# Third input-projection tile packed to 64 columns on two column halves, two inverses' stores moved from SyncE to GpSimd, six pieces of weight sums put into the cross-attention scores

## Chip, cores and metric

One core of a Trainium2 chip. The metric is the device time of one execution in microseconds (us): the median over runs of the whole layer, 512 tokens, model width 2048, float32 in and out.

## The reference, cut to what matters

```
h  = x
y  = rmsnorm(h) @ W_in                    # 7440 columns: GDN group and RWKV-7 group
h += concat[GDN(y_gdn), RWKV7(y_rwkv)] @ W_out
h += cross_attention(rmsnorm(h), rmsnorm(mem))   # 4 heads, 256 memory tokens
h += square(relu(rmsnorm(h) @ w_up)) @ w_down    # hidden 8192
out = rmsnorm(h)
```

Most of y's columns are queries, keys and values of the heads. A few are not: 64 + 64 + 160 low-rank columns that make RWKV's decay, its in-context rate and its output gate, and 8 + 8 columns that make GDN's decay and beta. Of the 160 gate columns 128 fill a tile; the other 32 and GDN's 16 share the next tile, 48 columns in all.

## The kernel before

Weights come in as 128-row tiles of 1024 columns (512 KB). Each is split on the chip into a high and a low float32r part (ScalarE casts the high part, VectorE subtracts), as are the activations, and a product is three fast products: high by high, high by low, low by high. The small matrices of the recurrences are multiplied in full float32, which TensorE runs as two passes and the profile lists as two records.

**Stage 1** (to 1114 us) is one program whose order is written out by a planner (`run`, with the costs of `cost` and `issue`): generators hand it instructions, and it issues the one that could start earliest by its own clocks, with ranks for ties. The engines then keep that order. `projections` makes 59 tiles of y (128 columns by 512 tokens, 16 x 3 products each), then the 16 tiles of the cross-attention's keys (`kp`), then 32 products that fold W_q into the keys (`kq`); these are dense work that is always at hand. Between them go the eight pairs of RWKV heads (`rwkv`) and the eight GDN heads (`gdn`), long chains of small products. Tiles 0 and 1 are made together; tile 2 is the one with 48 used columns. `evict` multiplies a finished tile by the row norm (`rstd`) and puts it into one of four buffers (`ybuf`). `rows` turns tiles 0 to 2 into the low-rank factors and GDN's decay and beta (R, its transpose RT, and its copy Rd in HBM, from which each head fetches its rows). x itself lies in sixteen tiles (`xr`) whose memory the heads take over later. `loader` keeps three raw weight tiles and three splits in flight.

Each head needs the inverse of a triangular matrix. `inverse_blocks` writes the matrix to HBM, GpSimd inverts all 16 x 16 diagonal blocks at once (4 x 16 or 4 x 8 blocks, one on each partition), SyncE stores the result T and its transpose U to HBM (`bg`), and loads them back in another layout; the levels above are small products. SyncE's queue, in order, also issues every weight load of the stage. The stores' blocks are runs of 16 numbers, 64 bytes.

**Stage 2** makes the values (`vp`, `vo`), the output projection (`op`), the scores (`sc`, two groups of eight steps of 24 products), the softmax and the attention (`at`). **Stage 3** is the MLP, both projections in a Strassen form with seven products for eight. The sums of w_down's blocks that this form needs (s1 to s4 of 14 groups, 2048 columns each) are made ahead by VectorE piece by piece: load four blocks, four sums, store four (`presum`). Stage 1 makes pieces of 410 columns when there is time, stage 3 makes the rest (`remaining`, `leftover`), in pieces of 512 and 256.

The packing is in `cost`, `loader`, `projections`, `shiftmix`, `rows` and one line of `gdn`; the stores are in `inverse_blocks`; the weight sums are in the loop over the scores. The lines that matter most:

```
yield TE.matmul(pt, wh[:, sl], his[k], start=(k == 0), stop=False)
yield TE.matmul(pt, wh[:, sl], los[k], start=False, stop=False)
yield TE.matmul(pt, wl[:, sl], his[k], start=False, stop=(k == nk - 1))
...
for t, b in (("T", Td), ("U", Ud)):
    yield SY.dma_start(views(bg[m, t])[1], b)
```

Of the kernel before, what the change touches and what calls it, by code (L numbers as in the profile page):

```python
# [73 lines left out]
def build(tc, I, out):  # L74
# [136 lines left out]
    def cost(op):  # L211
        eng, nm, _, a, k, out, ins, _ = op
        n = out.free_size()
        if eng == "PE":
            l = ins[0]
            if l.dtype == F32R:
                return n * 0.417 + (13.3 if state["shape"] is None else 120.0)
            sh = (l.partition_size(), l.free_size())
            sw = 0 if state["shape"] == sh or sh == (128, 128) else 100
            if nm == "transpose":  # L220
                return sw + (110 if sh[0] > 64 else 40)
            if sh == (64, 64):
                return sw + (32 if op[5].tensor.name[:2] in ("ri", "gi", "pa", "pv", "pu", "pw", "pk", "po", "pp") else 59)
            if sh[0] < 128 and n == 512:
                return sw + 530
            return sw + (115 if sh[0] < 128 and n == 128 else 2 * max(n * 0.84, 114))
# [159 lines left out]
    for n in range(2, NIN):  # L386
        wq += [("s", mem4[j]) for j in range(4) if n == NSQ[j]]
        wq += [("w", I["w_in"][n][:, h * 1024:(h + 1) * 1024]) for h in range(2)]
    kpo = [(0, 0), (1, 0), (0, 1), (1, 1)] + [(n, h) for n in range(2, KD) for h in range(2)]
# [33 lines left out]
    wq += [("w", I["wqT"][n][:, g * 1024:(g + 1) * 1024]) for n in range(KD) for g in range(2)]  # L423
    NKP, NKQ = 2 * NIN, 2 * NIN + 2 * KD
    raws, halves, used, whole, piece = {}, {}, set(), set(), {}
# [12 lines left out]
    def loader():  # L438
        w = nm = 0
        for i, (kind, _) in enumerate(wq):  # L440
            yield lambda: i in raws
            if kind == "w":
                if w in (2, 3):
                    hi, lo = (tile_of(pm, [P, 1024], F32R, t, f"w{t}", 1) for t in ("BK", "AR", "GA", "GB")[2 * w - 4:2 * w - 2])
                else:
# [3 lines left out]
                    hi, lo = halves[w] if w in piece else wsplit()  # L449
                if w in piece:  # L450
                    yield after("piece", w)
                    yield from split_(raws[i][:, 512:], hi[:, 512:], lo[:, 512:])
                else:
                    yield from split_(raws[i], hi, lo)
                    halves[w] = hi, lo
# [93 lines left out]
    def gemm_(pts, his, los, first, nk=KD, left=None):  # L549

        w = len(pts)
        for h in range(nk // 8):
# [15 lines left out]
            for j in range(w):  # L568
                used.add(first + h * w + j)

    khl = []

    def projections():
# [4 lines left out]
        for n in range(2, NIN):  # L578
# [9 lines left out]
            pt = psb(f"py{n}", "mm", 2)  # L588
            yield from gemm_([pt], xhi, xlo, 2 * n, left="x" if n == NIN - 1 else None)
            chain(evict(n, pt), 0)  # L590
# [63 lines left out]

    def shiftmix(n, mi, o):
        yield after("py", n)
        y = ybuf[ys[n]]
        yield AC.activation(o, y[:, 2:514], AF.Copy, scale=col("mu", mi))
        yield DV.scalar_tensor_tensor(out=o, in0=y[:, 3:515], scalar=omu[:, mi:mi + 1],
                                      in1=o, op0=ALU.mult, op1=ALU.add)  # L660
        yfree.append(ys.pop(n))
# [7 lines left out]
    def rows():  # L669
# [3 lines left out]
        g8 = slice(32, 40)  # L673
        b8 = slice(64, 72)
        yield after("rstd")
# [13 lines left out]
        events.add(("lowrank",))  # L689
        yield from shiftmix(2, 2, y2)  # L690
        yield AC.activation(y2[0:32, :], y2[0:32, :], AF.Tanh, scale=0.5)
        yield AC.activation(R[b8, :], y2[b8, :], AF.Tanh, scale=0.5)
        yield DV.tensor_scalar(out=y2[0:32, :], in0=y2[0:32, :], scalar1=0.5, scalar2=0.5,
# [27 lines left out]
        yield SY.dma_start(Rd, R[32:96, :])  # L721
        yield DV.tensor_copy(RT, pt.rearrange("p (c a b) -> p c a b", a=4, b=32)[:, :, 1:4, 0:8])

# [43 lines left out]
    def inverse_blocks(nm, store, m, tags, temps, ready, out, moved=False):  # L767
# [25 lines left out]
        for t, b in (("T", Td), ("U", Ud)):  # L793
            yield SY.dma_start(views(bg[m, t])[1], b)
        SM_ = Lane(nc.sync, "SP", wait=3000.0, margin=8000.0) if nm == "ri7" else SM
# [296 lines left out]
    def gdn(h):  # L1092
# [35 lines left out]
        if h == 0:  # L1128
            yield SL.dma_start(E, Rd[h:h + 1, :].broadcast_to([P, T]))
        yield SL.dma_start(B, Rd[32 + h:33 + h, :].broadcast_to([P, T]))  # L1130
        k_ = yield from conv(0, 1, "gk")
# [551 lines left out]
    def turned():  # L1683
        g, _, probs = turn.pop(0)
        for e in range(2):
            for mt in range(2):
# [5 lines left out]
                V.tensor_tensor(out=plo[kk], in0=pt, in1=phi[kk].bitcast(F32), op=ALU.subtract)  # L1692

    for g in range(2):
        banks = (("mm", 2), ("mg", 2), ("mg", 2), ("mm", 2)), (("scr", 1), ("scg", 1), ("mx", 2), ("mx", 2))
        pts = [psb(f"sc{g}_{t}", *banks[g][t]) for t in range(4)]
        for n2 in range(8):
# [4 lines left out]
            wh = pw.tile([P, 1024], F32R, tag="whi", name=f"kqh{cnt[0]}", bufs=NWS)  # L1702
            wl = pw.tile([P, 1024], F32R, tag="wlo", name=f"kql{cnt[0]}", bufs=NWS)
            split(raw, wh, wl)
            if g == 0 and n2 < 6:
                second(2 * n2 + 4)
# [16 lines left out]
        if g == 1:  # L1723
            for n in range(2):
                begun.append((psb(f"at{n}", "mg"), *wload(VOd[0][:, :, n * P:(n + 1) * P])))
                attend(*begun[n], 0)
        turn.append((g, pts, []))
        if g == 1:
# [653 lines left out]
def layout(inputs):  # L2382
# [8 lines left out]
    def tiles(w):  # L2391
# [8 lines left out]
    blocks = [w[:, o0:o0 + 128], w[:, o0 + 128:o0 + 256],  # L2400
              w[:, o0 + 256:o0 + 288], w[:, 4 * GW:4 * GW + 8], zero(24),
              w[:, 4 * GW + 8:4 * GW + 16], zero(56)]
    for j in range(8):
        s = slice(j * P, (j + 1) * P)
        blocks += [w[:, r0:][:, s], w[:, r0 + GW:][:, s], w[:, r0 + 2 * GW:][:, s]]
        blocks += [w[:, i * GW:][:, s] for i in (1, 0, 2, 3)]
    d["w_in"] = tiles(np.concatenate(blocks, 1))

    prm = np.zeros((P, NPRM), f)
# [70 lines left out]
```

## Time and profile before

| | us |
|---|---|
| median of 3 runs | 2887.0 |
| the runs | 2884.05 to 2889.67 |
| the profiled execution's own time | 2888.22 |
| its span, first to last instruction | 2886.4 |
| TensorE busy | 2863.3 |
| VectorE busy | 2333.2 |
| ScalarE busy | 1572.1 |
| GpSimd busy | 217.4 |

How to read it: busy times are of the span. Matmuls overlap, so one of 0.39 us may follow another after 0.23 us; what a product costs in a stream is the distance from one start to the next. PE is TensorE, DVE VectorE, ACT ScalarE, POOL GpSimd, SPq SyncE's queue. The mean granted TensorE clock of the run is 0.998 of full speed.

### The profile page before, as it was taken

The numbers are of one execution on the slowest core, as the hardware profiler recorded it, in microseconds if no ns is written. First come the engines' busy times: TensorE is split into PE (matmuls) and PEld (weight loads), VectorE is DVE, ScalarE is ACT, GpSimd is POOL, SyncE is SP. The second block draws the span as 40 slices with busy tenths as digits, with TensorE's granted clock in tenths as the row PEclk, the third lists the DMA queues.
The fourth block names the chain that finished last, engine by engine and source line by source line (L and its number), as shares of the span: only waits on it lengthen the run. The fifth ranks groups of instructions, "written<-read, shape, count | busy, mean of one in ns | idle before, by whom it ended". The sixth has DMA issues, their size and how long they took to land.

```text
span 2886.4 us, 49147 instructions
## 1 busy us (share of the span) xinstructions
PE 2863.3 (99%) x18794; PEld 2419.9 (84%) x18794; DVE 2333.2 (81%) x3559; ACT 1572.1 (54%) x2233; POOL 217.4 (8%) x539
## 2 busy tenths in 40 slices
PE   9999999999999999999999999999999999999998
PEld 7877877877877888889988888888888888888887
DVE  7787777787887877769946898899998878786888
ACT  6555555645655655664445556555555645454544
POOL 0313213213212200000000000000000000000000
PEclk9999999999999999999999999999999999999999
DMA  5656657556666788784323354666565878877733
GB/s 191 166 148 174 176 148 187 166 153 178 189 168 197 214 266 273 233 286 152 122 95 88 110 165 153 199 194 208 189 199 180 288 250 278 296 256 243 268 101 114
DMA packets 321213, 553.01 MB, mean 192 GB/s; under 512 B 101129, under 2 KB 188429, under 8 KB 320977
## 3 DMA queue, kind: packets, MB, share of 16 engines
q1 hardware_dynamic: 294592, 520.24, 58.7%
q10 hardware_dynamic: 26384, 29.63, 2.9%
q8 instruction: 147, 2.41, 0.3%
q14 instruction: 90, 0.73, 0.1%
HBM read 443.45 MB, written 106.31 MB: 190 GB/s over the span
## 4 chain that ended last, share of the span: by engine, by line
PE 95%; DMA 2%; DVE 1%; ACT 1%; issue 0%; ACTq 0%; SPq 0%; DVEq 0%
PE py L257 23%; PE mxu L257 12%; PE mgd L257 6%; PE mgu L257 6%; PE mxd L257 6%; PE op L122 6%; PE vp L122 3%; PE kp L257 3%; PE kq L257 3%; PE mmu L257 3%; PE sc L122 3%; PE at L122 3%; PE scgd L257 3%; PE scrd L257 3%; PE mmd L257 3%; PE vo L122 1%
## 5 line engine op out<-in xcount | busy, mean ns | idle before, releaser
L257 ACT CAST whi<-wraw 128x1024 fp32r<-128x1024 f32 (+1 forms) x365 | 382.8, 1049 | 367.2 <-PE py L257 136.2
L257 DVE TENSOR_TENSOR wlo<-wraw,whi 128x1024 fp32r<-128x1024 f32 (+1 forms) x365 | 446.4, 1223 | 92.5 <-ACT whi L257 86.2
L257 PE MATMUL py<-xhi,whi 128*128 128x512 f32 x928 | 373.5, 402 | 6.6 <-ACT xhi L257 6.6
L257 PE MATMUL py<-xhi,wlo 128*128 128x512 f32 x928 | 372.6, 402 | 0.0
L257 PE MATMUL py<-xlo,whi 128*128 128x512 f32 x928 | 372.0, 401 | 0.3 <-DVE xlo L257 0.3
L257 ACT CAST whi<-w 128x1024 fp32r<-128x1024 f32 x178 | 187.6, 1054 | 173.0 <-PE scgd L257 42.3
L257 DVE TENSOR_TENSOR wlo<-w,whi 128x1024 fp32r<-128x1024 f32 x178 | 217.3, 1221 | 43.2 <-ACT whi L257 41.2
L257 PE MATMUL mxu<-cb,whi 128*128 128x512 f32 x1016 | 249.3, 391 | 0.0
L257 PEld LDWEIGHTS mxu<-cb,whi 128*128 128x128 f32 x1016 | 184.7, 189 | 34.3
L257 PEld LDWEIGHTS py<-xhi,whi 128*128 128x128 f32 x928 | 175.0, 189 | 41.7 <-ACT xhi L257 6.9
L257 PEld LDWEIGHTS py<-xhi,wlo 128*128 128x128 f32 x928 | 175.1, 189 | 34.5 <-issue 1.0
L257 PEld LDWEIGHTS py<-xlo,whi 128*128 128x128 f32 x928 | 175.1, 189 | 34.2 <-DVE xlo L257 1.1
L131 DVE TENSOR_TENSOR wlo<-wraw,whi 128x1024 fp32r<-128x1024 f32 x112 | 136.7, 1222 | 44.3 <-ACT whi L130 43.8
L130 ACT CAST whi<-wraw 128x1024 fp32r<-128x1024 f32 x112 | 117.6, 1051 | 86.2 <-PE op L122 29.0
L257 PE MATMUL mxu<-cb,wlo 128*128 128x256 f32 x1016 | 142.7, 283 | 0.7 <-DVE wlo L257 0.7
L257 PEld LDWEIGHTS mxu<-cb,wlo 128*128 128x128 f32 x1016 | 135.1, 191 | 6.0 <-DVE wlo L257 0.9
L257 PE MATMUL mgu<-cb,whi 128*128 128x512 f32 x512 | 129.3, 394 | 0.1
L257 PE MATMUL mxd<-whi,cb 128*128 128x512 f32 x512 | 126.8, 389 | 0.0
L257 PE MATMUL mgd<-whi,cb 128*128 128x512 f32 x512 | 126.4, 389 | 0.0
L257 ACT ACT_TABLE_LOAD x87 | 111.6, 1283 | 16.3 <-DVE suml_gon L257 8.6
L122 PE MATMUL op<-ob,whi 128*128 128x256 f32 (+1 forms) x752 | 115.3, 304 | 0.0
L257 ACT CAST whi<-ws 128x1024 fp32r<-128x1024 f32 x75 | 78.9, 1053 | 63.8 <-PE mgu L257 47.9
(943 smaller groups left out, 6436.4 us busy)
## 6 DMA issues: line engine op xcount, KB each, us to landing
wraw<-in_w_in SPq DMA_DIRECT2D x116, 512.0 KB, 4.8
wraw<-in_w_up SPq DMA_DIRECT2D x65, 512.0 KB, 3.7
w<-in_w_up SPq DMA_DIRECT2D x63, 512.0 KB, 3.9
ds<-in_w_dm SPq DMA_DIRECT2D x128, 205.0 KB, 4.2
sd_s<-ds SPq DMA_DIRECT2D x128, 205.0 KB, 4.7
wraw<-sd_s SPq DMA_DIRECT2D x51, 512.0 KB, 4.8
w<-sd_s SPq DMA_DIRECT2D x50, 512.0 KB, 5.3
w<-in_w_dm SPq DMA_DIRECT2D x48, 512.0 KB, 5.0
```

Of the source, the lines that this page charges most:

```text
L122: PE.matmul(o, l, r, start=start, stop=stop, skip_group_check=again)
L130: S.copy(hi, src)
L131: V.tensor_tensor(out=lo, in0=src, in1=hi.bitcast(F32), op=ALU.subtract)
L257: f(*a, **k)
```

## The change

Three edits. (1) Tile 2's 48 used columns and 16 zeros are laid out as 64 columns by 16 row blocks in one weight tile instead of two. The product of row block k goes to column half k mod 2 of the array, in full float32 and with x unsplit, so that the low 64 partitions of the result sum the even blocks and the high 64 the odd; the eviction adds both. The norm's gain, else applied to x, is applied to the weights by one VectorE instruction, and the two splits of the tile are gone. `rows` waits until these products are issued, since its tiles take over x's memory. GDN's 16 rows lie side by side now, so beta's rows move from 32 to 40 in Rd, and RT is filled by two copies. (2) The stores of T and U of the last RWKV pair and the last GDN head are issued by GpSimd, in parts of 32 partitions: four and two transfers in place of two and two. (3) Six pieces of 256 columns of the weight sums are made in the scores' loop: 24 loads, 24 sums, 24 stores.

```
+            if sh == (128, 64) and n == 512:
+                return sw + 440
...
-        wq += [("w", I["w_in"][n][:, h * 1024:(h + 1) * 1024]) for h in range(2)]
+        wq += [("w", I["w_in"][n][:, h * 1024:(h + 1) * 1024]) for h in range(2 if n > 2 else 1)]
...
-                if w in piece:
+                if w == 4:
+                    c = lambda a: a.rearrange("p (k c) -> p k c", c=64)
+                    yield DV.tensor_tensor(out=c(hi.bitcast(F32)), in0=c(raws[i]),
+                                           in1=cols("norm_mix").unsqueeze(2).broadcast_to([P, KD, 64]), op=ALU.mult)
+                    halves[w] = hi, lo
+                elif w in piece:
...
+    def gemm_halves(pt, first):
+
+        yield half(first)
+        yield lambda: len(xhi) == KD
+        w = halves[first][0].bitcast(F32)
+        for k in range(0, KD, 2):
+            yield [TE.matmul(pt[i * 64:i * 64 + 64, :], w[:, (k + i) * 64:(k + i) * 64 + 64], xr[k + i],
+                             start=k == 0, stop=k == KD - 2) for i in (0, 1)]
+        used.add(first)
+        events.add(("few",))
+
+    def evict_halves(n, pt):
+        yield after("rstd")
+        yield lambda: bool(yfree)
+        b = yfree.pop(0)
+        t = short()
+        yield AC.copy(t[0:64, :], pt[64:128, :])
+        yield DV.tensor_tensor(out=t[0:64, :], in0=pt[0:64, :], in1=t[0:64, :], op=ALU.add)
+        yield DV.tensor_tensor(out=ybuf[b][0:64, 3:515], in0=t[0:64, :], in1=rstd[0:64, :], op=ALU.mult)
...
+            if n == 2:
+                yield from gemm_halves(pt, 4)
+                chain(evict_halves(n, pt), 0)
+                continue
...
-        b8 = slice(64, 72)
+        b8 = slice(64, 80)
+        yield after("few")
...
-            yield SY.dma_start(views(bg[m, t])[1], b)
+            if nm[2:] != "7":
+                yield SY.dma_start(views(bg[m, t])[1], b)
+                continue
+            for z in range(0, np_, 32):
+                yield GS.dma_start(views(bg[m, t])[1][z:z + 32], b[z:z + 32])
...
-        yield SL.dma_start(B, Rd[32 + h:33 + h, :].broadcast_to([P, T]))
+        yield SL.dma_start(B, Rd[40 + h:41 + h, :].broadcast_to([P, T]))
...
+    def fetched(s):
+        e, m, c, n = spans.pop(0)
+        b = [pl.tile([P, M], F32, tag=f"ds{i}", name=f"ds{s}_{i}", bufs=2)[:, 0:n - c] for i in range(4)]
+        for i in (A21, A22, A11, A12):
+            nc.sync.dma_start(b[i], I["w_dm"][e, m][i][:, c:n])
+        held.append((e, m, c, n, b))
+
+    def summed():
+        e, m, c, n, (a11, a21, a22, a12) = held.pop(0)
+        for j, o, x, y, op in (("s1", a22, a21, a22, ALU.add), ("s3", a21, a11, a21, ALU.subtract),
+                               ("s2", a11, a22, a11, ALU.subtract), ("s4", a12, a12, a11, ALU.subtract)):
+            V.tensor_tensor(out=o, in0=x, in1=y, op=op)
+            made_.append((Sd[e, m, j][:, c:n], o))
...
+            stored()
+            if g * 8 + n2 in (0, 2, 4, 6, 8, 10):
+                fetched(g * 8 + n2)
             split(raw, wh, wl)
+            if g * 8 + n2 in (2, 4, 6, 7, 12, 13):
+                summed()
```

`stored` issues the stores of the sums made since, from SyncE; `spans` lists what stage 1 left undone. The rest of the diff renumbers weight tiles by one, cuts `shiftmix` and two activations to the used rows, fills RT by two copies, and lays out the host's arrays.

## Rows read from the trace of the kernel before

**Rows 1.** the page's part 1: busy us, share of the span and instructions of each engine

```profile
PE 2863.3 (99%) x18794; PEld 2419.9 (84%) x18794; DVE 2333.2 (81%) x3559; ACT 1572.1 (54%) x2233; POOL 217.4 (8%) x539
```

**Rows 2.** whom TensorE waited for over the whole run: us in total, times, longest us

```profile
PE py L257 <- ACT xhi L257: 6.6, 1, 6.6
...
PE vo L122 <- DVE wlo L131: 0.9, 2, 0.8
```

**Rows 3.** timeline of TensorE: its one longer wait inside the run, in the key products

```profile
914.07 0.74 PE L257 MATMUL kp<-mhl,wlo 128*128 128x256 f32 x4 [3.23 <-DVE wlo L257]
```

**Rows 4.** timeline of TensorE (start us, us): third tile's first product, fourth's, a full-precision sum

```profile
31.43 0.39 PE L257 MATMUL py<-xhi,whi 128*128 128x512 f32 x1
...
42.32 0.39 PE L257 MATMUL py<-xhi,whi 128*128 128x512 f32 x1
42.55 1.02 PE L257 MATMUL pss<-r,cst 128*128 128x512 f32 x2
...
43.63 0.39 PE L257 MATMUL py<-xhi,wlo 128*128 128x512 f32 x1
```

**Rows 5.** timeline of TensorE: a pair of full-precision products on two row halves, between projection products

```profile
57.73 0.39 PE L257 MATMUL py<-xlo,whi 128*128 128x512 f32 x1
58.04 0.69 PE L257 MATMUL pW<-wa,lw 64*128 64x512 f32 x1
...
58.58 0.59 PE L257 MATMUL pW<-wa,lw 64*128 64x512 f32 x1
...
59.44 0.39 PE L257 MATMUL py<-xhi,whi 128*128 128x512 f32 x1
```

**Rows 6.** timeline of TensorE: four 64x64 products on the four quadrants, and the next four's first

```profile
111.11 0.22 PE L257 MATMUL pak<-BK,GA 64*64 64x64 f32 x1
...
111.12 0.22 PE L257 MATMUL pal<-BK,GA 64*64 64x64 f32 x1
...
111.17 0.22 PE L257 MATMUL pak<-BK,GA 64*64 64x64 f32 x1
```

**Rows 7.** timeline of VectorE: the first evictions of the projections

```profile
46.27 1.89 DVE L257 TENSOR_TENSOR y<-py,rstd 128x512 f32<-128x512 f32 x3 [1.67 <-ACT rstd L257]
```

**Rows 8.** timeline of SyncE's queue (start us, issue us) at the last RWKV inverse's stores

```profile
894.21 0.58 SPq L257 DMA_DIRECT2D bg16T<-sr  x1
894.89 0.61 SPq L257 DMA_DIRECT2D bg16U<-sr  x1
...
901.72 3.82 SPq L257 DMA_DIRECT2D E<-bg16U  x4
905.64 0.53 SPq L257 DMA_DIRECT2D wraw<-in_wk  x1
```

**Rows 9.** 2-us stretches: busy us (and count) of PE, PEld, DVE, ACT, POOL, then granted clock

```profile
914.00:916.00 2.00, 1.93 (x38) 1.71 (x38) 1.97 (x5) 2.00 (x4) 0.00 (x0) 0.72 0.38 127
916.00:918.00 2.00, 2.00 (x14) 1.64 (x7) 2.00 (x5) 0.54 (x1) 0.00 (x0) 0.50 0.72 225
918.00:920.00 2.00, 2.00 (x35) 1.64 (x37) 1.39 (x4) 0.54 (x2) 0.00 (x0) 0.93 0.81 264
```

**Rows 10.** timeline of GpSimd: the last GDN inverse, its first and last instruction

```profile
936.81 0.89 POOL L257 TENSOR_TENSOR sgj<-sgi 32x15 f32<-32x15 f32 x1 [41.52 <-DMA sgi<-ndgi]
...
953.57 1.68 POOL L257 COPY sgi<-sgi 32x256 f32<-32x256 f32 x1
```

**Rows 11.** products by tile: last RWKV output products (us of starts), products that wait for them

```profile
L257 PE MATMUL pp<-GA,BK x8: 218/218/218, 972.9 to 973.3; 64*64 64x64 f32 x8
...
L257 PE MATMUL kq<-khl,whi x256: 387/393/501, 1019.5 to 1113.2; 128*128 128x512 f32 x128
```

**Rows 12.** the scores, and 40 us of the MLP's up projection: columns as in rows 9

```profile
1453.00:1551.00 98.00, 97.76 (x450) 80.80 (x448) 43.95 (x77) 37.83 (x68) 0.00 (x0) 1.00 0.30 96
1960.00:2000.00 40.00, 40.00 (x242) 35.71 (x241) 36.40 (x48) 22.62 (x31) 0.00 (x0) 1.00 0.64 207
```

**Rows 13.** VectorE by form: weight sums of 256 columns (count, busy us, mean ns, idle us)

```profile
L257 DVE TENSOR_TENSOR h<-h 128x256 f32<-128x256 f32 x24 | 10.0, 418 | 0.1
```

More of the change, by code (lines that the diff above doesn't have):

```diff
@@ L423, in build @@
     wq += [("w", I["wqT"][n][:, g * 1024:(g + 1) * 1024]) for n in range(KD) for g in range(2)]
-    NKP, NKQ = 2 * NIN, 2 * NIN + 2 * KD
+    NKP, NKQ = 2 * NIN - 1, 2 * NIN - 1 + 2 * KD
     raws, halves, used, whole, piece = {}, {}, set(), set(), {}
@@ L569, in gemm_ @@
                 used.add(first + h * w + j)
+    def gemm_halves(pt, first):
[15 more added lines that the diff above has]
+        yield DV.tensor_tensor(out=ybuf[b][0:64, 3:515], in0=t[0:64, :], in1=rstd[0:64, :], op=ALU.mult)
+        ys[n] = b
+        events.add(("py", n))
     khl = []
@@ L588, in projections @@
             pt = psb(f"py{n}", "mm", 2)
-            yield from gemm_([pt], xhi, xlo, 2 * n, left="x" if n == NIN - 1 else None)
+            if n == 2:
+                yield from gemm_halves(pt, 4)
+                chain(evict_halves(n, pt), 0)
+                continue
+            yield from gemm_([pt], xhi, xlo, 2 * n - 1, left="x" if n == NIN - 1 else None)
             chain(evict(n, pt), 0)
@@ L653, in qevict, with shiftmix @@
         yfree.append(b)
-    def shiftmix(n, mi, o):
+    def shiftmix(n, mi, o, z=slice(0, P)):
         yield after("py", n)
         y = ybuf[ys[n]]
-        yield AC.activation(o, y[:, 2:514], AF.Copy, scale=col("mu", mi))
-        yield DV.scalar_tensor_tensor(out=o, in0=y[:, 3:515], scalar=omu[:, mi:mi + 1],
-                                      in1=o, op0=ALU.mult, op1=ALU.add)
+        yield AC.activation(o[z], y[z, 2:514], AF.Copy, scale=col("mu", mi)[z])
+        yield DV.scalar_tensor_tensor(out=o[z], in0=y[z, 3:515], scalar=omu[z, mi:mi + 1],
+                                      in1=o[z], op0=ALU.mult, op1=ALU.add)
         yfree.append(ys.pop(n))
@@ L689, in rows @@
         events.add(("lowrank",))
-        yield from shiftmix(2, 2, y2)
+        yield from shiftmix(2, 2, y2, slice(0, 64))
         yield AC.activation(y2[0:32, :], y2[0:32, :], AF.Tanh, scale=0.5)
-        yield AC.activation(R[b8, :], y2[b8, :], AF.Tanh, scale=0.5)
+        yield AC.activation(R[b8, :], y2[32:48, :], AF.Tanh, scale=0.5)
         yield DV.tensor_scalar(out=y2[0:32, :], in0=y2[0:32, :], scalar1=0.5, scalar2=0.5,
@@ L721, in rows @@
         yield SY.dma_start(Rd, R[32:96, :])
-        yield DV.tensor_copy(RT, pt.rearrange("p (c a b) -> p c a b", a=4, b=32)[:, :, 1:4, 0:8])
+        p4 = pt.rearrange("p (c a b) -> p c a b", a=4, b=32)
+        yield DV.tensor_copy(RT[:, :, 0:3:2, :], p4[:, :, 1:4:2, 0:8])
+        yield DV.tensor_copy(RT[:, :, 1, :], p4[:, :, 2, 8:16])
     hA, hB = HALF = slice(0, 64), slice(64, 128)
@@ L1692, in turned, with stored @@
                 V.tensor_tensor(out=plo[kk], in0=pt, in1=phi[kk].bitcast(F32), op=ALU.subtract)
+    spans = [(e, m, c, min(c + M, 2048)) for e, m in todo for c in range(upto.get((e, m, "s4"), 0), 2048, M)]
+    held, made_ = [], []
+    def fetched(s):
[10 more added lines that the diff above has]
+            made_.append((Sd[e, m, j][:, c:n], o))
+            upto[e, m, j] = n
+        if n == 2048:
+            todo.remove((e, m))
+    def stored():
+        while made_:
+            nc.sync.dma_start(*made_.pop(0))
     for g in range(2):
@@ L1726, in build @@
                 attend(*begun[n], 0)
+            stored()
         turn.append((g, pts, []))
@@ L2400, in layout @@
     blocks = [w[:, o0:o0 + 128], w[:, o0 + 128:o0 + 256],
-              w[:, o0 + 256:o0 + 288], w[:, 4 * GW:4 * GW + 8], zero(24),
-              w[:, 4 * GW + 8:4 * GW + 16], zero(56)]
+              zero(128)]
     for j in range(8):
@@ L2407, in layout @@
     d["w_in"] = tiles(np.concatenate(blocks, 1))
+    few = np.concatenate([w[:, o0 + 256:o0 + 288], w[:, 4 * GW:4 * GW + 16], zero(16)], 1)
+    d["w_in"][2, :, 0:1024] = few.reshape(16, P, 64).transpose(1, 0, 2).reshape(P, 1024)
     prm = np.zeros((P, NPRM), f)
```

## The prediction

> **What bounds the kernel now.** I read the busy times first: TensorE works 2863.3 of the span's 2886.4 us [rows 1], so 23.1 us are all that it leaves. Then whom TensorE waited for: 6.6 us at the start for the first activations [rows 2], 3.2 us once in the key products, until 914.07 [rows 3], and nothing else above 0.9 us [rows 2]; the other 13 us I take for the work after the last product and for waits under 1 us. So a stage is worth what TensorE does in it. Work on another engine counts only where it makes TensorE wait, and the one such place that the diff comes near is the wait of 3.2 us. Third, the distances between starts in TensorE's timeline: the duration of one product, 0.39 us, overlaps its neighbours and is no price. Tile 2's 48 products run from 31.43 to 42.32, 10.89 us, 0.227 each [rows 4]. That is the sum's first term.
>
> **Packing: what goes.** The 48 products go, 10.89 us of TensorE. Off its path one weight load of 512 KB goes, and two ScalarE casts with two VectorE subtractions.
>
> **Packing: what comes.** Sixteen full-precision products of 512 tokens, in eight pairs. The price of one with all 128 columns stands in the sum of squares: from 42.55 to 43.63 are that product and one projection product, so 1.08 - 0.227 = 0.85 us [rows 4]. No row has a product of 128 rows and 64 columns, so the pair is bounded. Below: both halves at once, 0.85 us a pair, 6.8 us for eight. Above: one after the other, 16 x 0.85 = 13.6 us. The nearest rows are the four quadrant products of the recurrence: they start within about 0.01 us of each other, and the next four 0.06 us later [rows 6], where at the price above (0.85/512, 1.67 ns a column for both passes) one pass of 64 columns takes 0.053 us. So four run at once, and `pak` and `pal` of GA, by the code, read the same row half and write different column halves with different moving data. That is what the change asks of the array, on all rows in place of half. I take the lower bound, and add the cost of changing the form: a pair on two row halves with one projection product before and one after takes 59.44 - 57.73 = 1.71 us [rows 5]; less 2 x 0.227 and 0.85 that is 0.40 us. The tile then costs 6.8 + 0.4 = 7.2 us, and TensorE has 10.9 - 7.2 = 3.7 us less to do.
>
> The page TensorE: Matmul & The Clock Gate of the Trainium skill (Part 3, The mechanism) says that a weight load runs beside products in flight only when its row group differs; two column halves share theirs. The quadrants speak against this reading, since they change weights every pass on the same rows without a gap. By that rule the gain would be the smaller one worked out next. The first pass of the row-half pair took 58.58 - 58.04 = 0.54 us for 0.43 [rows 5], 0.11 more; paid in all sixteen passes that is 1.8 us, and the gain is 1.9.
>
> Does the gain survive? The first evictions come at 46.27 to 48.16, when the norm is known [rows 7], no matter what TensorE does. Tile 4 needs tile 2's bank: tile 3 now starts at about 38.7 and ends, with the sum of squares in it, at 50.4. Evicting tile 2 takes a copy, a sum and a product where one instruction of 0.63 us stood; two more of that size put it at about 49.4. So tile 4 waits for nothing, with 1 us to spare; were the norm 3 us later, 2 of the 3.7 us would go. The wait on the event `few` costs nothing: the products are issued before the norm exists. The gain scaling and the extra eviction steps lie on VectorE and ScalarE, which TensorE never waits for there.
>
> **The stores.** Two issues of 0.58 and 0.61 us leave SyncE's queue [rows 8], and with them the queue's wait for GpSimd's result. GpSimd issues four transfers in their place (and two for the GDN head), and has nothing behind them: it sits idle for 41.5 us until the next block arrives [rows 10]. Who waits is SyncE again: the loads of T and U stand in its queue and need the stores landed, and behind the four U loads, 901.72 to 905.54, comes a key weight [rows 8], and TensorE's wait ends at 914.07 with the split of a key weight [rows 3]. So this is where the edit can pay or cost. No row has a transfer issued by GpSimd. If each took what SyncE's does, 0.6 us, U's second part would be out 4 x 0.6 us after the result, 1.2 us later than now, while the queue before it is 1.2 us shorter: nothing. Below: the planner, which counts 0.62 us for each, puts the loads after the weight, and the wait goes. With it goes its echo: after the wait the granted clock was 0.72, 0.50 and 0.93 in three stretches of 2 us [rows 9], the mixture of 1.2 and 2.4 GHz; shortfalls of 0.28, 0.50 and 0.07 times 2 us make 1.7 us. In all 4.9 us gained. Above: each transfer holds GpSimd as long as its longest instruction there, 1.68 us [rows 10]; then U is out 6.7 us after the result in place of 1.3, the weight comes 5.4 us later, and with a longer slow clock that is some 6 us lost. I take nothing, as the nearest row is SyncE's own store. RWKV's last chain itself has slack: its output products are done at 973.3, and the products that wait for them start at 1019.5, when the keys are finished [rows 11].
>
> The page SBUF — State Buffer of the Trainium skill (SBUF: two separate sides, the trap "DVE blocks DMA") says that GpSimd cannot write a transfer's descriptors while VectorE holds their shared port, and gives 3.1 us for a transfer that takes 0.62 alone. No row shows a GpSimd transfer; by that figure, as an estimate, four would lose 10 us. It points to the upper bound, and its case is the rival for slower below.
>
> **The weight sums.** In the scores VectorE is busy 43.95 and ScalarE 37.83 of 98 us, the DMA share is 0.30, and TensorE lacks 0.24 us [rows 12]. 24 sums at 0.418 us [rows 13] are 10 us of VectorE's 54 idle, and 48 transfers at 0.53 us of issue, a weight load's [rows 8], are 25 us of the 98 on a queue that otherwise only loads the scores' operands. The stores wait for sums made a step of 24 x 0.227 = 5.4 us earlier, and operands are three steps ahead: I cost it at nothing; without that cover one late operand would cost up to a step, 5.4 us. What is taken from the MLP gains nothing: TensorE is busy 40.00 of 40 us there [rows 12].
>
> **The sum.** -3.7 + 0 + 0. The profiled execution took 2888.2 us (2886.4 and 1.8 around it), 1.2 above the median of 2887.0, so it would come to 2884.5. Against the median: **2883.3 us**. A measurement of this kernel can tell some 0.2% from no change, 5.8 us here, so this forecast is inside what counts as the same.
>
> **The rivals.**
> - *The key products' wait goes too.* For it: two issues and a wait leave the queue ahead of the late weight. Against it: the U loads still stand ahead, unless the planner moves them. 2887.0 - 3.7 - 4.9 = 2878.4.
> - *The halves do not run together*, or only in part, with their weight loads in the open. For it: no row has 128 rows on a column half. Against it: the quadrants. From 2885.1 (weight loads exposed) to 2887.0 + 13.6 + 0.4 - 10.9 = 2890.1 (serial).
> - *The change does not do what it says:* the 3.7 us come back as a wait, at tile 4 or wherever the planner's new order has one. For it: the heads' first steps start when the norm is known, not when tile 2 is. Against it: TensorE waits nowhere between tile 2 and 910 for over 0.9 us. 2887.0.
> - *Slower: GpSimd's stores are late and SyncE's queue stands.* The loads of T and U wait at the head of the queue, the key weights behind them. There is no cover, since TensorE waits there already, so each us of delay is one lost. From 3.7 us it eats the gain; from 9.5 the kernel is slower by over 0.2%. With a delay of 12 us and 1.7 more of slow clock: 2897. For it: GpSimd's own instructions take up to 1.68 us there [rows 10], and no row shows what a transfer costs it. Against it: each of the four would have to take over 2 us.
>
> **How the numbers follow.** Forecast 0.42, the keys' wait gone 0.31, halves not together 0.08, gain given back 0.08, slower 0.11. Within the forecast another order of the planner moves the time by 2 or 3 us; 0.08 of it is beyond 5.8. Faster by over 0.2%: 0.30 of the second case and these 0.08, 0.38. Slower: 0.09 of the last. The same: 0.53. The range goes from 2877.5, below the second case, to 2890.5, above serial halves; it leaves out most of the slower case and the tails.
>
> **What would show it.** Right: tile 2 takes about 7.2 us with the two halves' products starting within 0.02 us of each other; tile 3 starts near 38.7; no new wait before 900; key products that wait 3 us or less; up projection at 40.00 of 40. Wrong: pairs 1.7 us apart, a wait of over 1 us before tile 4, SyncE waiting for GpSimd's stores ahead of key weights, or a wait in the scores.

## The result, and the profile after

The changed kernel takes 2893.2 us (median of 15 runs, 2887.9 to 2897.9) against 2888.9 us of the kernel before on the same chips (15 runs, 2884.1 to 2890.9): a ratio of 1.0020, 95% interval 1.0013 to 1.0027. The forecast was a gain of 3.7 us; it is a loss of 4 to 6: small, but the interval leaves 1 out, and the median lies above the range's top of 2890.5. The profiled execution took 2892.3 us, its span is 2890.6.

**Tile 2 does what it was to do.** TensorE's timeline of the changed kernel, the third tile (start us, us):

```profile
33.10 0.64 PE L259 MATMUL py<-gq,whi 128*64 128x512 f32 x1
33.11 0.64 PE L259 MATMUL py<-gk,whi 128*64 128x512 f32 x1
33.58 0.59 PE L259 MATMUL py<-gq,whi 128*64 128x512 f32 x1
...
40.12 0.50 PE L259 MATMUL py<-xhi,whi 128*128 128x512 f32 x1
```

The halves of a pair start 0.01 us apart, the pairs 0.43 us a pass (the first 0.48), and from the first product to tile 3's first are 40.12 - 33.10 = 7.02 us, where [rows 4] have 10.89: 3.87 us less. Across each of the two changes of form the distance is 0.33 us in place of 0.23; with both counted the gain is 3.7.

**The time is lost behind it, in stage 1.** Whom TensorE waited for in the changed kernel, which answers to [rows 2]:

```profile
PE py L259 <- ACT xhi L259: 7.7, 1, 7.7
PE ri7s L259 <- DVE k L259: 5.1, 1, 5.1
PE pkk L259 <- DVE gk L259: 2.3, 1, 2.3
PE kq L259 <- DVE y L259: 1.7, 1, 1.7
PE pwt L259 <- issue: 1.1, 1, 1.1
```

(`ri7s`, `pwt`, `pv` and `rs` are small products of the RWKV pairs, `pkk` and `gs` of the GDN heads.) The start's wait is of the run, not of the change (6.3 to 8.2 us in the profiles below, on any kernel). The other four are new, 10.2 us; before had 3.2 in the key products [rows 3] and nothing else above 0.9 [rows 2]. The starts of the later stages show where the loss arises (1.7 us of it lie ahead of tile 2, at 33.10 for 31.43):

| first product of | before | after | later by |
|---|---|---|---|
| vp | 1114.4 | 1119.8 | 5.4 |
| sc | 1453.1 | 1457.4 | 4.3 |
| mxu | 1632.6 | 1636.9 | 4.3 |
| span's end | 2886.4 | 2890.6 | 4.2 |

Two sums come near it, here and for most of the kernels below. The waits of TensorE between 30 us and the end of the keys (1130) are 5.3 us before and 11.5 after. The mean granted clock is 0.99870 over 137 executions of before and 0.99754 over 26 of the changed kernel, which over 2887 us is 3.8 and 7.1 us short of full speed (each clock has three decimals, and 0.001 is 2.9 us, so these means are rough). So -3.9 + 6.2 + 3.3 = 5.6 us, against 4 to 6 measured; about 1 us of it stands in both sums, as the clock falls within the wait already.

The longest new wait lies where the stores are. GpSimd's timeline, SyncE's queue, then ScalarE, VectorE and TensorE of the changed kernel:

```profile
912.96 0.82 POOL L259 DMA_DIRECT2D bg16T<-sr  x1
916.25 0.66 POOL L259 DMA_DIRECT2D bg16T<-sr  x1 [2.47 <-DMA lg<-in_g2b]
919.46 0.66 POOL L259 DMA_DIRECT2D bg16U<-sr  x1 [2.54 <-issue]
922.38 0.66 POOL L259 DMA_DIRECT2D bg16U<-sr  x1 [2.27 <-issue]
...
914.12 0.35 SPq L259 DMA_DIRECT2D wraw<-in_wk  x1
915.95 3.80 SPq L259 DMA_DIRECT2D r<-bg16T  x2
922.10 4.48 SPq L259 DMA_DIRECT2D E<-bg16U  x4
926.67 1.50 SPq L259 DMA_DIRECT2D wraw<-in_wk  x3
...
931.47 1.04 ACT L259 CAST whi<-wraw 128x1024 fp32r<-128x1024 f32 x1 [7.13 <-DMA wraw<-in_wk]
...
932.55 1.23 DVE L259 TENSOR_TENSOR wlo<-wraw,whi 128x1024 fp32r<-128x1024 f32 x1 [7.29 <-ACT whi L259]
...
934.36 0.41 DVE L259 TENSOR_TENSOR k<-ri7w,cst 128x256 f32<-128x256 f32 x1
...
934.50 0.48 PE L259 MATMUL ri7s<-k,E 64*64 64x64 f32 x4 [5.09 <-DVE k L259]
```

GpSimd's four transfers take 0.66 to 0.82 us of it each, but go out 2.9 to 3.3 us apart; SyncE's two were 0.7 apart [rows 8]. The two loads of T wait for the first two, the loads of U for the other two, and behind these the next key weight goes out at 926.67, 12.5 us after the one before. Its split on ScalarE starts at 931.47, VectorE's half at 932.55, and behind that, in VectorE's order, stands the `k` for which TensorE waits 5.09 us. The stretch in columns as in [rows 9], and the scores and 40 us of the up projection as in [rows 12]:

```profile
930.00:935.00 5.00, 0.50 (x10) 0.46 (x13) 2.43 (x5) 3.50 (x5) 0.00 (x0) 0.72 0.96 316
935.00:940.00 5.00, 5.00 (x72) 4.69 (x73) 3.58 (x6) 0.70 (x1) 0.00 (x0) 0.60 0.55 183
1457.40:1555.40 98.00, 97.76 (x449) 80.78 (x448) 52.18 (x100) 37.77 (x68) 0.00 (x0) 1.00 0.47 146
1960.00:2000.00 40.00, 40.00 (x238) 35.55 (x237) 36.15 (x48) 22.62 (x33) 0.00 (x0) 1.00 0.63 203
```

The granted clock falls to 0.72 and 0.60 around the wait; over 930 to 935, at 0.72, TensorE is busy for only 0.50 of the 5 us. The scores have 52.18 us of VectorE in place of 43.95 and still all of TensorE but 0.24 us; the up projection is at 40.00 of 40.

**One more line differs** that the prediction did not look at: the stores of weight sums that stage 1 makes (transfers up to 1115 us with their count; first the kernel before, then the changed one).

```profile
sd_s<-ds SPq DMA_DIRECT2D x128, 205.0 KB, 4.7
...
sd_s<-ds SPq DMA_DIRECT2D x32, 204.0 KB, 2.6
```

```profile
sd_s<-ds SPq DMA_DIRECT2D x120, 205.0 KB, 4.3
...
sd_s<-ds SPq DMA_DIRECT2D x28, 204.0 KB, 3.6
```

160 stores before, 148 after. The planner makes sums in what time its own clocks leave until the last key tile; the changed kernel's order leaves it less.

### The profile page after: what moved, and what is told of

Read it like the earlier page. It is cut to its first block, busy times and chain, and to the rows that moved or that the text cites. A ratio compares the mean times of both kernels' runs of the same rounds, so it can differ in the third digit from the quotient of the medians.

```text
span 2890.6 us, 49215 instructions
## 1 busy us (share of the span) xinstructions
PE 2861.2 (99%) x18778; PEld 2415.1 (84%) x18778; DVE 2332.8 (81%) x3572; ACT 1567.4 (54%) x2232; POOL 220.1 (8%) x545
## 4 chain that ended last, share of the span: by engine, by line
PE 93%; DMA 3%; DVE 2%; ACT 1%; issue 1%; POOL 1%; ACTq 0%; SPq 0%; DVEq 0%; POOLq 0%
PE py L259 22%; PE mxu L259 12%; PE mgd L259 6%; PE mgu L259 6%; PE mxd L259 6%; PE op L122 5%; PE vp L122 3%; PE mmu L259 3%; PE sc L122 3%; PE at L122 3%; PE scgd L259 3%; PE scrd L259 3%; PE mmd L259 3%; PE kq L259 3%; PE kp L259 2%; DMA wraw<-in_wo 1%
## 5 line engine op out<-in xcount | busy, mean ns | idle before, releaser
L259 PE MATMUL py<-xhi,whi 128*128 128x512 f32 x912 | 366.8, 402 | 7.7 <-ACT xhi L259 7.7
L259 PE MATMUL py<-xhi,wlo 128*128 128x512 f32 x912 | 365.9, 401 | 0.0
```

What stands on the lines that cost most here:

```text
L259: f(*a, **k)
```

## The experiments

All are ratios to the kernel before on the same chip, with 95% intervals; the expectations, which name the theories by letters, stand indented. "Packing" is edit 1, "stores" edit 2, "sums" edit 3; the last column is the count of sum stores in stage 1. Below, c560, c600, c640 and c680 are short for a_nopool_c560 and so on.

| label | kernel | ratio | interval | sums |
|---|---|---|---|---|
| c_after | the changed kernel again | 1.0016 | 1.0007 to 1.0025 | 148 |
| a_nopool | packing, sums | 1.0010 | 1.0001 to 1.0019 | 148 |
| a_nosums | packing, stores | 1.0057 | 1.0045 to 1.0070 | 148 |
| b_pack | packing | 1.0058 | 1.0046 to 1.0071 | 148 |
| b_pool | stores | 1.0017 | 1.0008 to 1.0026 | 156 |
| b_sums | sums | 0.9997 | 0.9988 to 1.0006 | 160 |
| b_told | none; planner's cost of tile 2 alone | 1.0107 | 1.0093 to 1.0120 | 140 |
| a_nopool_c560 | a_nopool, 560 ns a product | 0.9999 | 0.9991 to 1.0008 | 160 |
| a_nopool_c600 | the same, 600 ns | 1.0003 | 0.9994 to 1.0011 | 160 |
| a_nopool_c640 | the same, 640 ns | 1.0001 | 0.9993 to 1.0010 | 160 |
| a_nopool_c680 | the same, 680 ns | 1.0004 | 0.9995 to 1.0013 | 156 |
| b_pack_c560 | packing, 560 ns | 1.0001 | 0.9993 to 1.0010 | 160 |
| a_c560 | all three, 560 ns | 1.0006 | 0.9997 to 1.0015 | 156 |
| a_twice | c560 with tile 2 made twice | 1.0016 | 1.0007 to 1.0025 | 160 |
| b_pool_told | stores, planner told 3.2 us each | 1.0021 | 1.0012 to 1.0030 | 160 |
| b_pool8 | stores, in pieces of 16 partitions | 1.0016 | 1.0007 to 1.0025 | 156 |
| b_pool_gi7 | stores of the GDN head alone | 1.0002 | 0.9994 to 1.0011 | 156 |
| b_act | stores issued by ScalarE | 1.0007 | 0.9998 to 1.0016 | 156 |

### Each edit alone

The edits are the change's own hunks, left out or put in alone; for the stores:

```
-            if nm[2:] != "7":
-                yield SY.dma_start(views(bg[m, t])[1], b)
-                continue
-            for z in range(0, np_, 32):
-                yield GS.dma_start(views(bg[m, t])[1][z:z + 32], b[z:z + 32])
+            yield SY.dma_start(views(bg[m, t])[1], b)
```

a_nopool (the changed kernel with this undone):

> The changed kernel with the last two inverses' stores back on SyncE: packing and weight sums alone. Theory S (the stores cost it): the wait of ri7s (5.1 us after, and none before) goes, the time is the kernel's before less the packing's 3.7 to 3.9 us, a ratio of 0.9985 to 0.9995 once the small new waits elsewhere are taken off. Theory O (the new order of the planner costs it, wherever it leaves waits; the stores are free): 1.001 to 1.003 as the changed kernel.

b_pool (the kernel before with the opposite):

> The kernel before with only the stores of the last two inverses on GpSimd, in pieces of 32 partitions. Theory S: E<-bg16U is issued 6 to 9 us later than in the kernel before (901.7), the key weights behind it too, and TensorE waits 5 us and more longer between 905 and 945: ratio 1.002 to 1.003. Theory O: 1.000, within 0.0007.

b_pack and b_sums (the kernel before with the hunks of edit 1, and of edit 3):

> The kernel before with only the packed product. Theory S: 0.9985 to 0.9995 (3.9 us less in tile 2, less at most 3 us of new small waits in other places). Theory O: 1.001 to 1.003, with waits of 4 us and more in all before 1120 that the kernel before lacks, at pkk, pwt or kq.

> The kernel before with only the six pieces of weight sums in the scores. Both theories, and the prediction: 1.000 within 0.0007, the scores 90 us as before. A third theory, M (the sums cost it: their loads and stores delay the scores' or the up projection's weights): 1.001 to 1.002, and a wait of 2 us or more at sc, at or mxu.

Neither theory holds alone. The stores cost the kernel before 4.9 us (0.0017 of 2887), a little less than theory S has it; the packing with the sums and without the stores is slower too (1.0010), as O has it; and by itself it is 17 us slower, worse than anything expected. The sums are free on the kernel before. The three alone add up to 0.0017 + 0.0058 - 0.0003 = 0.0072, the whole change is 0.0016 to 0.0020: the edits are not terms of a sum.

b_pool, GpSimd's and SyncE's timeline, and TensorE's wait at the keys:

```profile
896.23 0.82 POOL L257 DMA_DIRECT2D bg16T<-sr  x1
898.87 0.66 POOL L257 DMA_DIRECT2D bg16T<-sr  x1 [1.82 <-issue]
904.16 0.65 POOL L257 DMA_DIRECT2D bg16U<-sr  x1 [4.63 <-DMA r<-bg16T]
908.20 0.65 POOL L257 DMA_DIRECT2D bg16U<-sr  x1 [3.39 <-issue]
...
907.91 3.90 SPq L257 DMA_DIRECT2D E<-bg16U  x4
911.90 0.55 SPq L257 DMA_DIRECT2D wraw<-in_wk  x1
...
918.33 1.65 PE L257 MATMUL kp<-mhl,wlo 128*128 128x256 f32 x6 [5.92 <-DVE wlo L257]
```

The loads of U go out 6.2 us later than in [rows 8], and so does the key weight behind them; the wait of [rows 3] grows from 3.23 to 5.92 us. vp starts 3.7 us late.

b_pack, the wait that makes the 17 us, in the down projection, and SyncE's queue ahead of it:

```profile
2748.71 2.08 PE L259 MATMUL scrd<-whi,cb 128*128 128x512 f32 x4 [9.18 <-ACT whi L259]
...
2733.45 3.19 SPq L259 DMA_DIRECT2D sd_s<-sl  x3
...
2740.22 1.55 SPq L259 DMA_DIRECT2D wraw<-sd_s  x3
```

(`scrd` is a product of the down projection.) vp is only 3.1 us late there and mxu 3.3; the other 14 us come here, 9.2 as the wait and the rest behind it, where the granted clock is 0.50 over 2745 to 2750 and 0.62 over the next 5 us. With 148 sum stores in stage 1 the rest is made in stage 3, and it is not done in time: the last sums are stored at 2733 to 2737, the weights that need them are loaded from 2740.22, and TensorE stands still until 2748.71.

### The sums in the changed kernel

a_nosums takes edit 3 out of the changed kernel (`fetched`, `summed` and `stored` with their calls):

> The changed kernel without the six pieces of sums in the scores. Theory N (its list makes 148 stores of sums in stage 1, and what is left comes too late for the last groups of the down projection): TensorE waits 7 us or more at scrd between 2700 and 2800, ratio 1.005 to 1.008. Rival (the sums in the scores change nothing here either, as on the kernel before): 1.0015 to 1.0025 and no such wait.

The theory holds: 1.0057, and the wait is there again, 9.60 us until 2749.89. So the sums, worth nothing on the kernel before, are worth 0.0057 - 0.0016 = 0.0041, 12 us, on the changed one: they make up for the 12 stores that its order leaves out. That is why a_nopool is 13 us faster than b_pack.

### Other orders, the same work

The planner's cost of a packed product is changed, and nothing else; in b_told, on the kernel before, that of an unpacked product of tile 2.

```
             if sh == (128, 64) and n == 512:
-                return sw + 440
+                return sw + 560
...
+                if out.tensor.name.split("_")[0] == "py2":
+                    return n * 0.285
                 return n * 0.417 + (13.3 if state["shape"] is None else 120.0)
```

> Packing and sums, stores on SyncE; the planner is told 560 ns for a packed product in place of 440, and with that list makes as many weight sums in stage 1 as the kernel before (160 stores of sums; 148 with 440). The instructions of the packed product are the same. Theory O (the packing gains its 3.9 us, and the planner's new list gives it back in waits and in sums not made): another list is another draw, and with all sums made in time 0.9975 to 1.0005. Theory D (the packed product itself, its eviction and its changes of form cost more than they save): 1.001, as with 440 ns.

> The same with 680 ns, so that the planner counts 10.9 us for tile 2 as it did before the change; 156 stores of sums in stage 1. Theory O: 0.998 to 1.001 by what waits its list has; the sum of new waits and half-clock stretches before 1120 accounts for its time. Theory D: 1.001.

> The kernel before, unpacked, with the planner alone told that tile 2's products take 3.9 us less: the list changes, the work does not. It makes 140 stores of sums in stage 1 where before made 160. Theory O: 1.004 to 1.012, partly in waits before 1120 and partly, as in the packing alone, in the down projection, which has 20 stores of sums more to make. Theory D: 1.000 within 0.0007.

> Packing and sums, stores on SyncE, planner told 600 ns: 160 stores of sums in stage 1. Theory O: 0.9975 to 1.0000, vp starting 2 to 4 us earlier than in the kernel before when both are counted from the first product. Rival G (the 3.9 us never reaches the end, whatever the list): 1.0000 to 1.0010.

> The same with 640 ns, 160 stores of sums as well: theory O 0.9975 to 1.0000, rival G 1.0000 to 1.0010.

> The packing alone (no sums in the scores, stores on SyncE), planner told 560 ns: 160 stores of sums in stage 1 as in the kernel before, where the packing alone with 440 ns made 148. Theory N (with 148 the sums left over come later than the last groups of the down projection need them): no wait of over 1 us at scrd and 0.9985 to 1.0008. Rival: the packing without the sums in the scores costs in itself: 1.004 or more, with 9 us at scrd.

b_told settles that an order alone can do it: not one product is changed, and the kernel is 31 us slower. In its profiled execution vp starts 11.4 us later than before and mxu 10.4, and the rest is lost in the down projection, as in b_pack:

```profile
PE scrd L259 <- ACT whi L259: 12.8, 2, 12.3
```
Theory D, that the packed tile costs more than it saves, has the 7.02 us and c560 against it, and b_pack_c560 shows the converse of b_told: the packing alone, on an order that leaves 160 sum stores, has no wait at scrd and is 17 us faster than b_pack.

But rival G holds as well. c560, c600, c640 and b_pack_c560 leave all sums where they were, and lie at 0.9999, 1.0003, 1.0001 and 1.0001; c680, with 156, at 1.0004. The first four keep nearly the same order in stage 1, so they are four measurements of one case. It is nearly the order of the kernel before, too: of the 9415 products that TensorE has there up to 1114 us, 9355 stand in the same sequence, by their tiles, in c560, and 7834 in the changed kernel. The packing's 3.9 us would be 0.9987, below every one of the intervals. The gain is made at 40 us and is not there at the end, and a new order is hardly what takes it.

a_twice asks where it goes:

```
-        for k in range(0, KD, 2):
+        for k in range(0, 2 * KD, 2):
...
-                return sw + 560
+                return sw + 280
```

with indices modulo KD, so that tile 2 is computed twice over itself.

> The kernel of 560 ns (packing and sums, stores on SyncE, 160 stores of sums in stage 1) with the packed product of tile 2 made twice, the second time over the first: 7.0 us more of TensorE in the same place, the planner told 280 ns a product, so that it counts the same time. Theory G (the packing's 3.9 us is given back in front of waits for VectorE, at rs near 815 and gs near 1030): the waits at these two shrink by 2 to 4 us in sum, and the time is 3 to 4 us above the kernel of 560 ns, 1.0010 to 1.0015. Rival (the gain is lost elsewhere, with no slack behind tile 2): all of the 7 us arrive, 1.0022 to 1.0030, and the two waits are as they were (3.9 us in sum).

TensorE's waits at two places of c560, which in the profile of the kernel before are nothing and 0.8 us:

```profile
816.03 0.43 PE L259 MATMUL rs<-BK,BTz 128*128 128x64 f32 x2 [1.50 <-DVE BK L259]
...
817.84 0.41 PE L259 MATMUL rs<-Qs,WTz 128*128 128x64 f32 x2 [0.70 <-DVE Qs L259]
...
1030.23 0.49 PE L259 MATMUL gs<-gEG,gq 128*128 128x128 f32 x2 [1.65 <-DVE gEG L259]
```

And of a_twice's waits, the longest after the start and the only one at those places:

```profile
PE kp L259 <- ACT mhl L259: 1.4, 1, 1.4
...
PE rs L259 <- DVE Qs L259: 0.8, 1, 0.8
```

With work put back into tile 2, 3.9 us at these places become 0.8 (823.87 us), but 1.4 us at the keys and others are new: from 30 us on, 6.4 us of waits become 6.0. Nor do these places tell of the packing. b_sums, whose stage 1 is that of the kernel before with tile 2 at its full price, waits there too:

```profile
PE gs L257 <- DVE gEG L257: 1.2, 1, 1.2
PE rs L257 <- DVE Qs L257: 1.0, 1, 1.0
PE rs L257 <- DVE BK L257: 0.6, 1, 0.6
```

The profiled executions of b_sums, c560 and a_twice have the full granted clock (1.00) from tile 2's first product to vp, and take 1081.6, 1079.1 and 1086.9 us for it: of the 3.9 us that c560 saves 2.5 arrive, and for the 6.9 that a_twice puts back it is 7.8 us later. So the slack of theory G is not shown. a_twice's time lies between the two expectations with an interval that takes in both, and doesn't decide either. What is left is the balance of the two sums:

| kernels | tile 2 | waits, 30 to 1130 | clock, us short | sum | measured |
|---|---|---|---|---|---|
| before | | 5.3 | 3.8 | | |
| c560, c600, c640, b_pack_c560 | -3.9 | 6.4, 7.0, 9.4, 8.2 | 5.5 (45 runs) | +0.2 | +0.3 |
| a_twice | +3.0 | 6.0 | 5.2 | +5.1 | +4.6 |
| a_nopool | -3.9 | 9.9 | 5.2 | +2.1 | +2.9 |
| b_pool | 0 | 8.3 | 6.3 | +5.5 | +4.9 |
| b_pool8 | 0 | 9.2 | 5.2 | +5.3 | +4.6 |
| a_c560 | -3.9 | 8.0 | 6.8 | +1.8 | +1.7 |
| a_nopool_c680 | -3.9 | 6.4 | 3.7 | -2.9 | +1.2 |
| b_pool_told | 0 | 12.4 | 6.0 | +9.3 | +6.1 |
| the changed kernel | -3.9 | 11.5 | 7.1 | +5.6 | +4.6 to +5.8 |

(Waits from one profiled execution of each kernel, the clock from all; sums and measured times in us against before. Waits of 5.3 are one execution's too: b_sums and b_pool_gi7, with the same tile 2, have 4.9 and 6.0. About 1 us of the changed kernel's sum and 1.7 of b_pool's are slow clock within a wait, counted twice.) Two rows miss by 3 to 4 us: a_nopool_c680's profiled execution was 3 us faster than its median, b_pool_told's 7 us slower, so one execution's waits don't stand for all. With that reserve, on an order that leaves all sums, some 2.4 us of the packing's 3.9 come back as waits and 1.7 as slow clock, an estimate from the table. Which waits, and why they grow, isn't settled; most are for VectorE.

### The stores

> The kernel before with the stores on GpSimd and the planner told that each takes GpSimd 3.2 us: its list puts two key weights ahead of the loads of U on SyncE. Theory Q (the stores cost because the key weights stand in SyncE's queue behind loads that wait for them): 0.9990 to 1.0007 and no wait at kp above 3.3 us. Rival C (the stores cost by their transfers, whatever stands behind them): 1.0017 as without the telling; rival O again: other waits of 2 us and more in other places.

> The kernel before with the stores on GpSimd in pieces of 16 partitions in place of 32, so eight for the last ri and four for the last gi. Theory P (each transfer that GpSimd issues holds up the next for some 3 us, whatever its size): the eight start 20 to 30 us from first to last, E<-bg16U is issued after 918 and the time is 1.004 or more. Theory B (the gap goes by what a transfer carries): 1.5 us apart and the last 9 to 12 us after the first, as with four pieces: 1.0017.

> The kernel before with those stores issued whole by ScalarE. Theory S (what costs is that GpSimd's pieces go out 3 to 5 us apart): both stores out within 1.5 us of the result, E<-bg16U issued within 1.5 us of where it was (901.7), 0.9990 to 1.0007. Rival: taking them from SyncE's queue costs in itself, by the list that it brings: 1.0012 to 1.0025.

> The kernel before with only the last gi's two stores on GpSimd. Theory S (the loss is at the last ri, where the key weights stand behind its loads): 0.9992 to 1.0008 and at most 3.3 us at kp. Rival: gi7's stores carry their share: 1.0010 to 1.0020 and a new wait between 955 and 1000.

The edits: `3200 if eng == "POOL"` in the planner's clock for transfers; `range(0, np_, 16)`; `AC.dma_start` in place of GpSimd's loop; `nm != "gi7"` in place of `nm[2:] != "7"`.

The loss is at the last ri: with the GDN head's stores alone it is 1.0002, though its interval just meets b_pool's. Telling the planner the true price doesn't help. It puts two key weights ahead of the loads of U, as meant, but GpSimd's transfers then go out up to 5.8 us apart, and the four loads of U hold SyncE's queue from 914.87 to 922.36. b_pool_told, GpSimd:

```profile
903.94 0.66 POOL L257 DMA_DIRECT2D bg16T<-sr  x1 [1.79 <-issue]
909.76 0.65 POOL L257 DMA_DIRECT2D bg16U<-sr  x1 [5.16 <-DMA mraw<-in_memT]
```

The wait at the keys is 4.1 us, and other waits (4.8 us at `rs`) come with the order: 1.0021. Theory Q falls, as an improvement at least.

b_pool8 decides between P and B. GpSimd's timeline with pieces of half the size:

```profile
896.34 1.84 POOL L257 DMA_DIRECT2D bg16T<-sr  x3
899.41 0.57 POOL L257 DMA_DIRECT2D bg16T<-sr  x1 [1.23 <-issue]
900.03 1.12 POOL L257 DMA_DIRECT2D bg16U<-sr  x2
905.49 1.12 POOL L257 DMA_DIRECT2D bg16U<-sr  x2 [4.34 <-issue]
```

The first three go out 0.6 us apart, then come gaps of 1.2 and 4.3 us, and the eighth is out at 906.6, 10.3 us after the first; the four of b_pool took 12.6. So the number of transfers doesn't set the time, and theory P falls; theory B has the total, but not the even spacing. When the stores land tells more. In the changed kernel (size, median us from issue to landing):

```profile
bg16T<-sr POOLq DMA_DIRECT2D x2, 32.0 KB, 2.9
bg16U<-sr POOLq DMA_DIRECT2D x2, 32.0 KB, 2.8
```

Its first three stores land at 915.93, 919.15 and 922.08, and the next go out at 916.25, 919.46 and 922.38; in b_pool they land at 898.55, 903.85 and 907.90, and the next go out at 898.87, 904.16 and 908.20. In all kernels whose GpSimd stores 32 partitions at a time (512 runs of 64 bytes), each further store of an inverse goes out 0.30 to 0.32 us after the one before has landed, 25 times of 25. In b_pool8 (256 runs) three are out at once; the fourth goes 0.31 us after the first has landed, the seventh 0.31 us after the fourth. No row names a landing as what GpSimd waited for; it is the times that agree. Issued by ScalarE, both stores are out within 1.5 us:

```profile
894.55 0.67 ACTq L257 DMA_DIRECT2D bg16T<-sr  x1
895.32 0.70 ACTq L257 DMA_DIRECT2D bg16U<-sr  x1
```

Yet the loads of U go out at 904.03, 2.3 us later than in [rows 8] and past the 1.5 us expected, behind those of T, and b_act is at 1.0007, with 1 inside its interval.

> The changed kernel itself, beside the next three on the same chip: 1.002, and after GpSimd's last store of the last inverse TensorE waits 5 us for ri7s and runs at 0.6 to 0.7 of its clock in that stretch, as in its first profile.

> The changed kernel, GpSimd's stores and all, with the planner told 560 ns for a packed product (156 stores of sums in stage 1; with SyncE's stores 160). Theory S (the stores on GpSimd cost 2 to 5 us on any list): 1.0007 to 1.0018, against 0.9999 with the stores on SyncE. Theory O (the stores cost nothing but the list they bring): 0.9990 to 1.0005.

On the changed kernel's own order the stores' share can't be told from the timing alone: 1.0016 to 1.0020 with them, 1.0010 without, and the intervals overlap. In the profiles TensorE gets its `k` at 934.50 with them and at 935.15 without, since a_nopool waits there too (2.3 us at `kp`, 1.6 at `ri7s`). A second pair on that order, without the sums, shows no share: 1.0057 with the stores (a_nosums) and 1.0058 without (b_pack). By the two sums it is 2 to 3 us, an estimate. On the order of c560 it is 1.0006 against 0.9999, with intervals that overlap: TensorE waits 7.04 us at the keys where c560 waits 1.5, but 1.0 us elsewhere up to 1130 where c560 waits 4.8.

No kernel beats the one before by more than its interval; b_sums, 0.9997, is the nearest.

## Why the prediction was wrong

- **What bounds the kernel:** right. TensorE is busy 99% of the span, and the loss is in its waits and its clock, as far as the two sums reach, and in sums not made.
- **Packing, its price:** right. 7.02 us for 7.2, and 3.87 gained for 3.7 (3.7 too with both changes of form). The quadrants of [rows 6] were the row to go by. By the page TensorE: Matmul & The Clock Gate of the Trainium skill (Part 3, The mechanism), read as the prediction did, weight loads would lie open on column halves; the pairs at 0.43 us a pass show none of the 0.11 us that the row-half pair had.
- **"Does the gain survive?": the step that failed.** It was followed to tile 4 and no further, and so far it was right. Behind that the text went by "TensorE waits nowhere between tile 2 and 910 for over 0.9 us", and took this as proof that TensorE sets the pace there. It was one execution's waits: b_sums, with the same stage 1, has two waits of 1.6 us in all near 817 in its own. The runs show in its place that on nearly the same order the 3.9 us are not there at the end (0.9999 to 1.0003 four times); by the sums some 2.4 come back as waits and 1.7 as slow clock, which the prediction counted for the stores and not here. What makes TensorE wait more stays open; that it gets ahead of VectorE is not shown. The rival "the 3.7 us come back as a wait" had 0.08 and comes nearest.
- **The new order: mis-sized.** "Another order of the planner moves the time by 2 or 3 us": it moved it by 31 us in b_told, where the planner is told wrong by 3.9 us, and by 17 between b_pack and b_pack_c560. The missing path is the sums: they fill what the order leaves in stage 1, and the last groups of the down projection need them by 2740.
- **The weight sums, "I cost it at nothing":** right on the kernel before, 0.9997, and "what is taken from the MLP gains nothing" too, by the row read. Wrong in the changed kernel, where they save 12 us. A term read from the kernel before was used beside another edit that changes what it rests on.
- **The stores, "I take nothing, as the nearest row is SyncE's own store":** wrong on the kernel before by 4.9 us, inside the upper bound of 6. The mechanism was the slower rival's, and the queue stood as it says: loads of U 6.2 us late, the wait of [rows 3] up by 2.7 us, and more slow clock. The price of a transfer was the term that failed: they go out 2.6 to 5.3 us apart in place of 0.6, each after the one before has landed. In the changed kernel itself their share isn't resolved.
- The page SBUF — State Buffer of the Trainium skill (SBUF: two separate sides, "DVE blocks DMA") gave about the right size, an estimate of 10 us more for four: from the first start to the last are 9.4 us after and 12.0 in b_pool, where three steps of 0.62 are 1.9, so 7.5 and 10.1 more. Its reason isn't borne out: the next store follows the landing of the one before by 0.3 us in all 25 cases; three pieces go out 0.6 us apart in b_pool8 beside a busy VectorE, and in b_pool VectorE is idle for 1.46 us in the middle of the gap from 899.53 to 904.16:

```profile
902.47 0.69 DVE L257 TENSOR_TENSOR gkn<-gk,sg 128x512 f32<-128x512 f32 x1 [1.46 <-ACT sg L257]
```

The account of the changed kernel, then, as an estimate: 3.9 us gained at tile 2; 6.2 more in waits and 3.3 more in slow clock, of which some 4 come with the packing on the order before as well, and the other 5 with this order and the stores, whose shares the runs don't separate; and 12 us lost to sums not made, which the sums in the scores give back.

## What to carry to other kernels

Where a planner writes the order, an edit is priced as the work and a new order: time the kernel before with the planner's cost changed and the work left alone, to see what an order by itself can do. A gain of a few us on an engine that is busy 99% of the time need not reach the end: waits and slow clock can take it back, and the waits of one execution don't tell which, since the same order waits elsewhere in the next. Profile the same order more than once before a wait is called absent. And count the filler work (here sums made in spare time), since what an order leaves out is paid elsewhere.

## What the runs showed of the hardware

- Two full-precision products of 128 rows by 64 columns run at once on the two column halves: starts 0.01 us apart, 0.43 us a pass of 512 columns, 0.86 a pair.
- Small stores issued by GpSimd (32 partitions, 32 KB in 512 runs of 64 bytes) occupy it for 0.65 to 0.82 us but go out 2.6 to 5.8 us apart, 0.30 to 0.32 us after the one before has landed, 25 times of 25. Of half that size three are out at once, 0.6 us apart.
- After the wait of 5.09 us the granted clock was 0.60 of full speed over 935 to 940, a mixture of 1.2 and 2.4 GHz, with TensorE busy 5.00 of the 5 us.
